# A layer kernel on one core: queries and keys stored split, and three output tiles moved beside the last attention head

## The chip, the cores and the metric

The kernel runs on one core of a Trainium2 chip. A core has five engines that work at the same time and each execute their own list of instructions strictly in order: TensorE (PE, matrix products), VectorE (DVE), ScalarE (ACT), GpSimd (POOL) and SyncE (SP, which here only issues transfers). They wait for each other through semaphores. The metric is the device time of one execution in microseconds, as the median of several.

## The reference, cut to what matters

One transformer-like layer over x (1024 tokens of 1024 numbers) and mem (256 tokens), all in float32:

```python
h = rms_norm(x, mix_pre_g)
u, q, k, v, f_logit = split(h @ w_in)            # 512 | 8 heads x 64, three times | 8
y_ssm = s5_mixer(u, ...)                         # state-space scan, gelu, gated linear unit
y_fox = forgetting_attention(q, k, v, f_logit)   # causal softmax attention with a decay bias
y_mix = concat([rms_norm(y_ssm, ssm_out_g), rms_norm(y_fox, fox_out_g)])
x = x + rms_norm(y_mix @ w_out, mix_post_g)
h = rms_norm(x, xa_pre_g)
x = x + rms_norm(memory_cross_attention(h, rms_norm(mem, mem_g), xa_wq, xa_wkv, xa_wo), xa_post_g)
h = rms_norm(x, ffn_pre_g)
x = x + rms_norm((silu(h @ w_gate) * (h @ w_up)) @ w_down, ffn_post_g)
```

## The kernel before, in words

**Precision.** Each factor of a product is split into a high part (a copy to the format fp32r, on ACT, L114) and the remainder (a subtraction on DVE, L116, or with a gain L118); `split` does this. `mm3` (L123 to L125) then makes one product out of three: high x high, high x low, low x high. So every operand costs ACT and DVE an instruction before PE may use it.

**Stages.** From 0 to about 185 us the input projection: u, then k, v, q in tiles of 128 columns by 1024 tokens (`qk_tile`, evacuated by L289), with the constants of the state-space branch (SSM) computed beside it on DVE (L505 to L621). To 222 the SSM's output (L638). From 222 to 500 the attention (`fox`). From 500 to 580 the output projection and the rest of the cross-attention's preparation, to 772 the cross-attention, to 1195 the first two products of the feed-forward part, and then the last.

**Attention.** `fox` goes through 64 units: 8 heads of 8 token tiles t, each of 128 rows against the 128(t+1) columns that causality leaves. A unit is: scores on PE (L734, L735), with a causal mask added (L737), into one of two two-bank PSUM buffers s; bias and minimum on DVE (L741); exponential on ACT (L743); reciprocal (L744) and normalisation, on DVE (L748) or, for t = 1, 3, 5 of heads 2 to 7, on POOL (L746); two units later transposes on PE (L765), evacuated by ACT or DVE (L770, L768); and after every pair of tiles of two heads the values' product (L779), whose squares are added up in `totals` (L789 to L793). `prepare(h)` loads one head's q and k from DRAM (qk_d, L714 and L715) in halves, and splits them: ACT L718 and L114, subtractions L719 and L116 on DVE for heads 0 and 1, on POOL for the others.

**Work beside it.** `fillers` is a second generator of PE work: the rest of v, the gated linear unit (`glu`), the SSM half of the output projection (`out_ssm`, L845, whose weights are in_w_out_s and whose result goes to DRAM as t1_d by L849), the memory tokens' normalisation (`mem_load`, L967), their 16 key and value tiles (`mem_tile`, evacuated by L979, stored as kv_d by L980), and `build_a(0)`, half of the product of the cross-attention's query weights with the keys. `paced` steps it at RATE steps per unit:

```python
    def paced(main, *side):
        for n, _ in enumerate(main):
            for gen, first, rate in side:
                if n >= first:
                    step(gen, int((n + 1 - first) * rate) - int((n - first) * rate))
```

Behind the attention come the attention half of the output projection (weights w_out_f[0] to [3], loaded by L1034 into the two buffers raw; eight token tiles; L1054 adds t1 back, L1062 adds the residual), and between its half tiles steps of `build_a(1)`.

**What sets the order.** The program is written as such generators, and a scheduler then fixes one order for each engine from the order of the code, priorities and the buffers that are free: raw has 2 buffers, whl (split weights) 3, slab 16, g in PSUM 4, s 2; t2 3, and a, b two each in the pool of temporaries, e and d one. `behind()` holds an instruction back until the last exponential that the code has issued. What the order doesn't move is waited for on the chip. Weights and reloaded intermediates are loaded through SP's queue, stores go through POOL's, except for t1_d and kv_d, which SP stores.

Of the kernel before, what the change touches and what calls it, by code (L numbers as in the profile page):

```python
# [17 lines left out]
P = 128  # L18
# [17 lines left out]
POOL_T = (1, 3, 5)  # L36
RATE = 1.02
# [4 lines left out]
OPB = 10  # L42
WARM = 11
# [10 lines left out]
def layer(ctx: ExitStack, tc: tile.TileContext, a, out):  # L54
# [95 lines left out]
    stA, stB, stC = pool, sp, pool  # L150
# [4 lines left out]
    def load_w(src, shape, first=0, stage=None):  # L155
        w = tt(stage, [P, D]) if stage else raw([P, D])
        hl = whl([P, 2, D])
        if not first:
            sp.dma_start(out=w, in_=src)
# [19 lines left out]
    qk_d = dram.tile([8, P, S], F32, name="qk_d")  # L179
# [105 lines left out]
    def qk_tile(i, xH, xL, rb, ahead=False):  # L285
        o = tt("a")
# [6 lines left out]
        stA.dma_start(out=qk_d[i], in_=o)  # L293
# [402 lines left out]

    def fox(yf):
        heads, units, pts = {}, {}, {}
        sv = const.tile([P, NT], F32, name="sv_f")

        def prepare(h):
            r0 = (h % 2) * 64
            qs = tt("a", [P, S], F32R)
            ka = slab([P, 2, S])
            ncb = tt("b")
            sp.dma_start(out=ncb, in_=nc_d[h:h + 1, :].broadcast_to([P, S]))
            heads[h] = (qs, ka, ncb)
            eng = dve if h < 2 else pool
            for hf in range(2):
                hs = slice(hf * 512, hf * 512 + 512)  # L710
                qk = tt("d" if h == 0 and hf else "e", [P, 2, 512])
                qd, kd = qk[:, 0], qk[:, 1]
                for rr in (0, 64):
                    sp.dma_start(out=qd[rr:rr + 64], in_=qk_d[h // 2, r0:r0 + 64, hs])  # L714
                    sp.dma_start(out=kd[rr:rr + 64], in_=qk_d[4 + h // 2, r0:r0 + 64, hs])  # L715
                yield
                with behind():
                    act.activation(out=qs[:, hs], in_=qd, func=AF.Copy)  # L718
                    eng.tensor_tensor(out=qs[64:128, hs], in0=qd[64:128], in1=qs[64:128, hs].bitcast(F32),  # L719
                                      op=ALU.subtract)  # L720
                    split(ka[:, 0, hs], ka[:, 1, hs], kd, lo_eng=eng)

        def behind():
            return tc.issue_after(last[-1].ins) if last else ExitStack()

        def scores(h, t):
# [18 lines left out]
            if t in POOL_T and h > 1:  # L745
                pool.tensor_tensor(out=sc[:, :ke], in0=sc[:, :ke], in1=rl.broadcast_to([P, ke]), op=ALU.mult)  # L746
            else:
                dve.tensor_scalar(out=sc[:, :ke], in0=sc[:, :ke], scalar1=rl, scalar2=None, op0=ALU.mult)  # L748
# [23 lines left out]
        def values(hp, qc):  # L772
# [28 lines left out]
        totals = []  # L801
# [22 lines left out]
        token_sums(sv, totals[0])  # L824
        rsqrt_mean(r_f, sv, 512)
# [133 lines left out]
    def mem_load(r, out):  # L959
# [23 lines left out]
    def fillers():  # L983
# [13 lines left out]
        yield from build_a(0)  # L997
# [3 lines left out]
    def build_a(c):  # L1001
        for t in range(2):
            Ah[c, t], Al[c, t] = slab([P, 4, 512]), slab([P, 4, 512])
        for h in range(2):
# [3 lines left out]
            kh = tt("ea"[h * (1 - c)], [P, 2, 2, 256], F32R)  # L1008
# [3 lines left out]
            for ft in range(0, KT, 2):  # L1012
# [611 lines left out]
```

## Time and profile before

| | |
|---|---|
| median of 3 runs | 1417.2 us (1416.4, 1417.2, 1421.53) |
| the profiled execution: its own time | 1418.95 us |
| its span, first to last instruction | 1417.2 us |
| mean granted clock of TensorE | 0.990 |

By stage, from windows of the trace (us of busy time; clock is the granted share of TensorE's full clock):

| stage | us | PE | DVE | ACT | POOL | clock |
|---|---|---|---|---|---|---|
| input projection, 0 to 185 | 185 | 182.2 | 151.8 | 89.0 | 11.4 | 1.00 |
| SSM output, to 222 | 37 | 35.9 | 8.3 | 16.5 | 3.4 | 1.00 |
| attention, to 500 | 278 | 259.9 | 185.8 | 182.3 | 65.2 | 0.96 |
| output projection, to 580 | 80 | 75.2 | 62.9 | 49.0 | 27.0 | 0.98 |
| cross-attention, to 772 | 192 | 191.5 | 101.6 | 72.7 | 23.3 | 1.00 |
| gate and up, to 1195 | 423 | 422.5 | 306.1 | 156.5 | 253.8 | 1.00 |
| down, to the end | 222 | 214.9 | 132.1 | 92.6 | 19.2 | 0.99 |

In the profile's rows an instruction is named by its engine, its line in the kernel and its operands as out<-in with the program's tile names; xN counts instructions. "idle before <-releaser" is the time in which the engine stood still ahead of it, and the instruction or transfer (DMA) that ended this.

### The profile page before, as it was taken

Reading aid. Unit: us, or ns where it says so; the run is one execution under the profiler, and the core shown is the slowest. Engines: PE = TensorE matmul, PEld = TensorE weight load, DVE = VectorE, ACT = ScalarE, POOL = GpSimd, SP = SyncE. Lnnn points to the kernel's source line nnn. Section 1 sums busy time; section 2 is a strip of 40 time slices with the busy share of each in tenths; the row PEclk is TensorE's granted clock in tenths of the full one; section 3 lists DMA queues with packets and bytes.
Section 4 is the critical chain, followed back from the end, with each engine's and each line's share of the span. In section 5 each row is a group of like instructions: output and inputs, shape, how many; then the busy total and the mean of one; then the engine's idle time right before and its main releaser. Section 6 shows DMA issues by size and latency. Waiting matters only on the chain.

```text
span 1417.2 us, 20364 instructions
## 1 busy us (share of the span) xinstructions
PE 1382.1 (98%) x7353; PEld 1162.5 (82%) x7353; DVE 948.5 (67%) x1693; ACT 658.7 (46%) x1305; POOL 403.2 (28%) x424
## 2 busy tenths in 40 slices
PE   9999999899899898999999999999999999999997
PEld 7889898689789686888888888888888888888886
DVE  8939937946566677636457677777776676555566
ACT  7372347866566555434334533333333334544441
POOL 0001000113243134002021467676666661000021
PEclk9999999899999999999999999999999999999999
DMA  6225554246543756024457255554444546955544
GB/s 216 91 90 136 156 179 130 75 148 188 182 129 103 198 178 220 15 75 148 164 179 266 98 186 186 185 186 149 149 156 156 171 149 234 346 207 191 180 163 164
DMA packets 109366, 231.07 MB, mean 163 GB/s; under 512 B 11720, under 2 KB 46536, under 8 KB 109136
## 3 DMA queue, kind: packets, MB, share of 16 engines
q1 hardware_dynamic: 94064, 178.34, 39.4%
q0 software_dynamic: 15200, 51.42, 10.2%
q8 instruction: 58, 0.95, 0.3%
q14 instruction: 44, 0.36, 0.1%
HBM read 165.23 MB, written 73.14 MB: 168 GB/s over the span
## 4 chain that ended last, share of the span: by engine, by line
PE 59%; DVE 1%; ACT 0%; issue 0%; DVEq 0%; ACTq 0%
PE x L1289 17%; PE g L1289 13%; PE x L1552 7%; PE g L1552 7%; PE x L125 2%; PE x L124 2%; PE x L123 2%; PE g L123 2%; PE g L125 2%; PE g L124 2%; PE g L1074 1%; PE g L1185 1%; DVE slab L116 0%; DVE whl L116 0%; DVE c L1062 0%
## 5 line engine op out<-in xcount | busy, mean ns | idle before, releaser
L1289 PE MATMUL x<-slab,op 128*128 128x512 f32 x984 | 233.2, 389 | 0.5 <-DVE op L116 0.5
L1289 PEld LDWEIGHTS x<-slab,op 128*128 128x128 f32 x984 | 184.6, 188 | 39.3 <-DVE op L116 1.0
L1289 PE MATMUL g<-slab,op 128*128 128x512 f32 x744 | 178.7, 389 | 0.0
L116 DVE TENSOR_TENSOR slab<-slab 128x1024 fp32r<-128x1024 f32 (+2 forms) x92 | 110.3, 1207 | 86.7 <-ACT slab L114 84.8
L1289 PEld LDWEIGHTS g<-slab,op 128*128 128x128 f32 x744 | 139.6, 188 | 29.0
L123 PE MATMUL g<-slab,whl 128*128 128x512 f32 (+1 forms) x416 | 151.7, 365 | 1.1 <-ACT t L979 0.7
L125 PE MATMUL g<-slab,whl 128*128 128x512 f32 (+1 forms) x416 | 148.7, 358 | 0.0
L124 PE MATMUL g<-slab,whl 128*128 128x512 f32 (+1 forms) x416 | 148.4, 357 | 0.0
L114 ACT ACTIVATE slab<-slab 128x1024 fp32r<-128x1024 f32 (+2 forms) x92 | 94.9, 1037 | 106.3 <-DMA slab<-hs_d 82.7
L1552 PE MATMUL g<-slab 128*128 128x512 f32 x462 | 126.6, 389 | 0.0
L1552 PE MATMUL x<-slab 128*128 128x512 f32 x462 | 126.6, 389 | 0.0
L1552 PEld LDWEIGHTS x<-slab 128*128 128x128 f32 x462 | 86.7, 188 | 18.0
L1552 PEld LDWEIGHTS g<-slab 128*128 128x128 f32 x462 | 86.7, 188 | 18.0
L116 DVE TENSOR_TENSOR whl<-raw,whl 128x1024 fp32r<-128x1024 f32 (+2 forms) x61 | 71.1, 1168 | 36.7 <-ACT whl L114 36.5
L116 DVE TENSOR_TENSOR op<-slab,op 128x512 fp32r<-128x512 f32 x80 | 86.4, 1091 | 11.6 <-ACT op L114 11.4
L123 PE MATMUL g<-whl,slab 128*128 128x256 f32 (+2 forms) x288 | 86.1, 307 | 5.0 <-ACT t L845 3.4
L123 PEld LDWEIGHTS g<-slab,whl 128*128 128x128 f32 x416 | 78.6, 189 | 12.2 <-ACT t L979 0.9
L125 PEld LDWEIGHTS g<-slab,whl 128*128 128x128 f32 x416 | 78.4, 189 | 11.8 <-DVE whl L116 0.2
L1365 POOL TENSOR_TENSOR wt<-wt 128x256 f32<-128x256 f32 x88 | 81.8, 930 | 19.6 <-DMA wt<-in_w_down 16.1
L124 PEld LDWEIGHTS g<-slab,whl 128*128 128x128 f32 x416 | 78.6, 189 | 10.6
L114 ACT ACTIVATE op<-slab 128x512 fp32r<-128x512 f32 x80 | 50.0, 627 | 78.5 <-PE x L1289 36.8
L124 PE MATMUL g<-whl,slab 128*128 128x256 f32 (+2 forms) x288 | 85.7, 298 | 0.0
(389 smaller groups left out, 2930.7 us busy)
## 6 DMA issues: line engine op xcount, KB each, us to landing
hs_d<-ev POOLq DMA_DIRECT2D x77, 256.0 KB, 2.6
slab<-hs_d SPq DMA_DIRECT2D x35, 512.0 KB
wt<-in_w_down SPq DMA_DIRECT2D x44, 256.0 KB
wt_d<-wt POOLq DMA_DIRECT2D x22, 512.0 KB, 4.7
slab<-in_w_gate SPq DMA_DIRECT2D x20, 512.0 KB
slab<-in_w_up SPq DMA_DIRECT2D x20, 512.0 KB
slab<-wt_d SPq DMA_DIRECT2D x20, 512.0 KB
wd_d<-in_w_down SPq DMA_DIRECT2D x33, 256.0 KB
```

The lines of the kernel that those rows point to most:

```text
L114: first = act.activation(out=hi, in_=src, func=AF.Copy, scale=1.0 if mul is None else mul)
L116: (lo_eng or dve).tensor_tensor(out=lo, in0=src, in1=hi.bitcast(F32), op=ALU.subtract)
L123: pe.matmul(ps, lh, rh, start=first, stop=False)
L124: pe.matmul(ps, lh, rl, start=False, stop=False)
L125: pe.matmul(ps, ll, rh, start=False, stop=last)
L1074: pe.transpose(tp[:, k], src[:, (k0 + k) * P:(k0 + k + 1) * P], ident)
L1185: turned = pe.transpose(tp[:, k], h3[:, (4 * n + k) * P:(4 * n + k + 1) * P], ident)
L1289: pe.matmul(ps, x[:, k], y[:, k], start=first and k + n == 0, stop=k == 3 and n == 2, skip_group_check=not first)
L1365: pool.tensor_tensor(out=o, in0=x, in1=y, op=ALU.subtract)
L1552: pe.matmul(banks[n][j], xo[:, u, js], wo[:, v], start=ends[0] and k == 0, stop=ends[1] and k == 2, skip_group_check=onto is not None)
```

## The change

1. `qk_d` holds q and k split, 2 x 128 x 1024 for each tile in place of 128 x 1024. `qk_tile` splits each half tile (high part into a t2 buffer, remainder in place) and stores three pieces, not one, through POOL's queue. `prepare` is left with loads alone: two for q, two for k per head.
2. `POOL_T` goes: DVE does all normalisations (now L743).
3. `stB` is POOL: the 32 stores of t1_d and kv_d leave SP's queue.
4. The weights w_out_f (`out_weights`) and the first three output tiles, 3, 4 and 5 (`out_tiles`), are now the last steps of `fillers`, each begun once the last head has given the token tiles that it needs (`ready`). The token sums are formed by parts (`out_scale`), and the end of a tile (`out_finish`) is written apart, for the first three behind the attention. `build_a(0)` is gone from the fillers; `both_a` runs both halves between the remaining five tiles.
5. `behind()` now also holds back the memory tokens' scaling and split (now L962), the splits of w_out_f and of build_a's products, and a few staged loads. The totals move to buffer e, as do all key splits of build_a; RATE is 0.98.

```diff
-POOL_T = (1, 3, 5)
-RATE = 1.02
+RATE = 0.98
...
+OUT_ORDER = (3, 4, 5, 6, 7, 0, 1, 2)
+EARLY = 3
...
-    stA, stB, stC = pool, sp, pool
+    stA, stB, stC = pool, pool, pool
...
-            sp.dma_start(out=w, in_=src)
+            with behind() if stage else ExitStack():
+                sp.dma_start(out=w, in_=src)
...
+    qk_d = dram.tile([8, 2, P, S], F32, name="qk_d")
...
     def qk_tile(i, xH, xL, rb, ahead=False):
-        o = tt("a")
+        hl = tt("a", [P, S], F32R)
+        o = hl.bitcast(F32)
...
         yield from proj_tile(load_w(a["w_f"][i], P), xH, xL, evac, ahead)
-        stA.dma_start(out=qk_d[i], in_=o)
+        for h in range(2):
+            hs = slice(h * 512, h * 512 + 512)
+            hi = t2t([P, 512], F32R)
+            split(hi, hl[:, hs], o[:, hs])
+            stA.dma_start(out=qk_d[i, 0, :, hs], in_=hi.bitcast(F32))
+        stA.dma_start(out=qk_d[i, 1], in_=o)
...
+    def behind():
+        return tc.issue_after(last[-1].ins)
...
-            eng = dve if h < 2 else pool
-            for hf in range(2):
...
-                    sp.dma_start(out=qd[rr:rr + 64], in_=qk_d[h // 2, r0:r0 + 64, hs])
-                    sp.dma_start(out=kd[rr:rr + 64], in_=qk_d[4 + h // 2, r0:r0 + 64, hs])
-                yield
-                with behind():
-                    act.activation(out=qs[:, hs], in_=qd, func=AF.Copy)
-                    eng.tensor_tensor(out=qs[64:128, hs], in0=qd[64:128], in1=qs[64:128, hs].bitcast(F32),
-                                      op=ALU.subtract)
-                    split(ka[:, 0, hs], ka[:, 1, hs], kd, lo_eng=eng)
-        def behind():
-            return tc.issue_after(last[-1].ins) if last else ExitStack()
+            q, k = qs.bitcast(F32), ka.bitcast(F32)
+            for t in range(2):
+                sp.dma_start(out=q[t * 64:t * 64 + 64], in_=qk_d[h // 2, t, r0:r0 + 64])
+            for rr in (0, 64):
+                sp.dma_start(out=k[rr:rr + 64], in_=qk_d[4 + h // 2, :, r0:r0 + 64].rearrange("t p s -> p t s"))
...
-            if t in POOL_T and h > 1:
-                pool.tensor_tensor(out=sc[:, :ke], in0=sc[:, :ke], in1=rl.broadcast_to([P, ke]), op=ALU.mult)
-            else:
-                dve.tensor_scalar(out=sc[:, :ke], in0=sc[:, :ke], scalar1=rl, scalar2=None, op0=ALU.mult)
+            dve.tensor_scalar(out=sc[:, :ke], in0=sc[:, :ke], scalar1=rl, scalar2=None, op0=ALU.mult)
...
-                    totals.append(tt("d"))
+                    totals.append(tt("e"))
...
-            split(yf[hp][:, 0, qs_], yf[hp][:, 1, qs_], yp, g_out[:, 4 + hp:5 + hp])
+            hi = split(yf[hp][:, 0, qs_], yf[hp][:, 1, qs_], yp, g_out[:, 4 + hp:5 + hp])
+            if (hp, qc) == (3, 3):
+                last.append(hi)
...
-        drain(prepare(0))
+        prepare(0)
...
-                    nxt = prepare(h + 1)
-                if t % 2 and h + 1 < NH:
-                    step(nxt)
+                    prepare(h + 1)
...
-        token_sums(sv, totals[0])
-        rsqrt_mean(r_f, sv, 512)
+                    if h == NH - 1:
+                        ready.append(t // 2)
...
             for kk in range(4):
-                dve.tensor_tensor(out=m[:, kk], in0=m[:, kk], in1=rb, op=ALU.mult)
-                split(mh[:, k + kk], ml[:, k + kk], m[:, kk], g_mem[:, k + kk:k + kk + 1])
+                with behind():
+                    dve.tensor_tensor(out=m[:, kk], in0=m[:, kk], in1=rb, op=ALU.mult)
+                    split(mh[:, k + kk], ml[:, k + kk], m[:, kk], g_mem[:, k + kk:k + kk + 1])
                 if kk % 2:
...
         yield from rows
-        yield from build_a(0)
+        yield from out_weights()
+        yield from out_tiles(OUT_ORDER[:EARLY], 0)
...
-            kh = tt("ea"[h * (1 - c)], [P, 2, 2, 256], F32R)
+            kh = tt("e", [P, 2, 2, 256], F32R)
             split(kh[:, 0], kh[:, 1], kr)
...
-                for f in range(2):
-                    split(Ah[c, ft // 4][:, ft % 4 + f, ms], Al[c, ft // 4][:, ft % 4 + f, ms], ps[:, f],
-                          g_xa[:, ft + f:ft + f + 1])
+                with behind():
+                    for f in range(2):
+                        done = split(Ah[c, ft // 4][:, ft % 4 + f, ms], Al[c, ft // 4][:, ft % 4 + f, ms], ps[:, f],
+                                     g_xa[:, ft + f:ft + f + 1])
                 yield
...
-    gp = fillers()
-    paced(fox(yf), (gp, 0, RATE))
-    drain(gp)
-    two.close()
-    psx = ctx.enter_context(tc.tile_pool(name="psx", bufs=4, space=PSUM))
+        last.append(done)
+    wo, kept, totals, ready, summed, unfinished = [], {}, [], [], [], []
+    sv_f = const.tile([P, NT], F32, name="sv_f")
...
-        return psx.tile(shape, F32, name="x", tag="x")
-    wo = []
-    for i in range(4):
-        w = raw([P, D])
-        sp.dma_start(out=w, in_=a["w_out_f"][i])
-        hl = slab([P, 2, D])
-        split(hl[:, 0], hl[:, 1], w)
-        wo.append(hl)
...
-    a1 = build_a(1)
-    kept = {}
-    for n, j in enumerate((3, 4, 5, 6, 7, 0, 1, 2)):
...
+    def out_weights():
+        g_mp.append(gain_row(0, "d"))
+        for i in range(4):
+            w = raw([P, D])
+            sp.dma_start(out=w, in_=a["w_out_f"][i])
+            hl = slab([P, 2, D])
+            with behind():
+                split(hl[:, 0], hl[:, 1], w)
+            wo.append(hl)
+        yield
+    def out_scale(j):
+        g = max(j // 2, 1)
+        if g not in summed:
+            summed.append(g)
+            js = slice(0 if g == 1 else 2 * g, 2 * g + 2)
+            token_sums(sv_f[:, js], totals[0][:, js.start * P:js.stop * P])
+            rsqrt_mean(r_f[:, js], sv_f[:, js], 512)
+    def out_tiles(order, n0):
+        for n, j in enumerate(order, n0):
+            while max(j // 2, 1) not in ready:
+                yield
+            ts = slice(j * P, (j + 1) * P)
+            t = tt("aba"[n % 3])
+            for i in range(2):
+                sp.dma_start(out=t[64 * i:64 * i + 64], in_=t1_d.rearrange("j (k s) d -> s k j d", s=16)[2 * j + i])
+            ss4 = sm(4, "ss4")
+            for h in range(2):
+                hs = slice(h * 512, h * 512 + 512)
+                ps = x_ps([P, 512])
+                for k in range(4):
+                    mm3(ps, yf[k][:, 0, ts], yf[k][:, 1, ts], wo[k][:, 0, hs], wo[k][:, 1, hs], k == 0, k == 3)
+                out_scale(j)
+                dve.scalar_tensor_tensor(out=t[:, hs], in0=ps, scalar=r_f[:, j:j + 1], in1=t[:, hs], op0=ALU.mult, op1=ALU.add)
+                for q in range(2 * h, 2 * h + 2):
+                    act.activation(out=tt("yt", [P, 256]), in_=t[:, q * 256:q * 256 + 256], func=AF.Square,
+                                   accum_out=ss4[:, q:q + 1])
+                pool.tensor_tensor(out=t[:, hs], in0=t[:, hs], in1=g_mp[0][:, hs], op=ALU.mult)
+                if h == 0:
+                    yield
+            unfinished.append((j, t, ss4))
+            if psx:
+                out_finish()
+            yield
+    def out_finish():
+        j, t, ss4 = unfinished.pop(0)
...
-        t = tt("aab"[n % 3])
...
-            step(a1)
+        sp.dma_start(out=xt, in_=a["x"][j * P:(j + 1) * P, :])
...
+    def both_a():
+        yield from build_a(0)
+        yield from build_a(1)
+    psx, g_mp = None, []
+    gp = fillers()
+    paced(fox(yf), (gp, 0, RATE))
+    two.close()
+    psx = ctx.enter_context(tc.tile_pool(name="psx", bufs=4, space=PSUM))
+    drain(gp)
+    for j in (4, 6):
+        out_scale(j)
+    while unfinished:
+        out_finish()
+    a1 = both_a()
+    for _ in out_tiles(OUT_ORDER[EARLY:], EARLY):
+        step(a1)
     drain(a1)
```

How this moves the instructions is seen in each engine's order; lines of the changed kernel have other numbers (its L1030 is L1034 of before, L1003 L1007, L1052 L1047, L1075 L1044, L161 L159; L117 is L116, L119 L118, L624 to L627 are L616 to L619, L292 is L289, L739 L741, L962 L967).

First, SP's queue near the end of the attention, before: raw is a load of weights, the names with t1 and kv_d are the intermediates read back, b, a, c and t2 their buffers.

```order
L849 DMA t1_d_112<-t2_4930 128x2x256
L1034 DMA raw_5371<-in_w_out_f 128x1024
L1047 DMA b_5596<-t1_d_112 64x1x1024 x2
L1007 DMA t2_5621<-kv_d_113 128x2x256
L1220 DMA t2_6027<-kv_d_113 128x2x256
L1047 DMA a_5395<-t1_d_112 64x1x1024 x2
L1047 DMA b_5850<-t1_d_112 64x1x1024 x2
L1034 DMA raw_5376<-in_w_out_f 128x1024
L1220 DMA t2_6078<-kv_d_113 128x2x256
L1044 DMA c_5393<-in_x 128x1024
L1044 DMA c_5503<-in_x 128x1024
```

And in the changed kernel, the same place:

```order
L1030 DMA raw_5011<-in_w_out_f 128x1024
L1030 DMA raw_5016<-in_w_out_f 128x1024
L720 DMA a_4244<-qk_d_107 64x1024 x2
L716 DMA b_4246<-nc_d_111 128x1024
L722 DMA slab_4245<-qk_d_107 64x2x1024 x2
L720 DMA a_4571<-qk_d_107 64x1024 x2
L716 DMA b_4573<-nc_d_111 128x1024
L722 DMA slab_4572<-qk_d_107 64x2x1024 x2
L1003 DMA t2_5395<-kv_d_113 128x2x256
L1003 DMA t2_5592<-kv_d_113 128x2x256
L1052 DMA a_5088<-t1_d_112 64x1x1024 x2
L1052 DMA b_5187<-t1_d_112 64x1x1024 x2
```

Two of the four loads of w_out_f (L1030) now stand ahead of the loads for heads 6 and 7 (a, b, slab from qk_d and nc_d); the other two stand farther down, behind loads of t1_d for the output tiles.

Second, DVE's queue at the second head, before; L967 scales the memory tokens (raw), L741 is the reduction of the scores s:

```order
L967 TENSOR_TENSOR raw_2774<-raw_2774,t2_2736 128x256 x3
L678 SCALAR_TENSOR_TENSOR t2_2672<-t2_2671,t2_2672 128x512
L967 TENSOR_TENSOR raw_2774<-raw_2774,t2_2736 128x256
L967 TENSOR_TENSOR raw_2879<-raw_2879,t2_2736 128x256 x4
L741 ISA c_2821,nlr_2822<-s_2815,b_2282 128x768
L741 ISA nlr_2822 128x1
L118 SCALAR_TENSOR_TENSOR slab_2773<-raw_2774,gains_98,slab_2772 128x256 x3
L118 SCALAR_TENSOR_TENSOR slab_2604<-t2_2672,gains_98,slab_2604 128x512
L684 TENSOR_TENSOR d_2342<-d_2342,t2_2671 128x512
```

And changed (L962 scales, L739 reduces):

```order
L739 ISA c_2814,nlr_2815<-s_2808,b_2304 128x768
L739 ISA nlr_2815 128x1
L742 RECIPROCAL nlr_2769<-nlr_2769 128x1
L686 SCALAR_TENSOR_TENSOR t2_2721<-t2_2720,t2_2721 128x512
L962 TENSOR_TENSOR raw_2828<-raw_2828,t2_2780 128x256 x4
L962 TENSOR_TENSOR raw_2935<-raw_2935,t2_2780 128x256
L743 TENSOR_SCALAR c_2768<-c_2768,nlr_2769 128x640
L962 TENSOR_TENSOR raw_2935<-raw_2935,t2_2780 128x256 x3
L742 RECIPROCAL nlr_2815<-nlr_2815 128x1
```

The reduction of the 768-wide tile stood behind all eight scalings, and now stands ahead of them.

Third, DVE's queue at the end of the input projection, before; L616 to L619 belong to the SSM, L289 evacuates q, L116 splits weights (whl):

```order
L616 TENSOR_TENSOR b_1668<-c_121,c_123 128x896
L116 TENSOR_TENSOR whl_1892<-raw_1891,whl_1892 128x1024
L617 TENSOR_TENSOR b_1669<-c_121,c_123 128x896
L618 TENSOR_TENSOR b_1668<-b_1668,b_1669 128x896
L289 SCALAR_TENSOR_TENSOR a_1821<-g_1827,d_690 128x4x128
L619 TENSOR_TENSOR b_1668<-b_1668,slab_938 128x896
L289 SCALAR_TENSOR_TENSOR a_1821<-g_1853,d_690 128x4x128
L116 TENSOR_TENSOR whl_2333<-raw_2331,whl_2333 128x1024
```

And changed; L117 with operands a and t2 is a split of q:

```order
L117 TENSOR_TENSOR whl_1956<-raw_1955,whl_1956 128x1024
L626 TENSOR_TENSOR b_1692<-b_1692,b_1693 128x896
L117 TENSOR_TENSOR a_1810<-a_1810,t2_1868 128x512
L117 TENSOR_TENSOR a_1810<-a_1810,t2_1872 128x512
L627 TENSOR_TENSOR b_1692<-b_1692,slab_953 128x896
L624 TENSOR_TENSOR b_1700<-c_121,c_123 128x896
L292 SCALAR_TENSOR_TENSOR a_1877<-g_1883,d_690 128x4x128
L625 TENSOR_TENSOR b_1701<-c_121,c_123 128x896
L626 TENSOR_TENSOR b_1700<-b_1700,b_1701 128x896
L292 SCALAR_TENSOR_TENSOR a_1877<-g_1909,d_690 128x4x128
L627 TENSOR_TENSOR b_1700<-b_1700,slab_954 128x896
L117 TENSOR_TENSOR whl_2396<-raw_2394,whl_2396 128x1024
```

The two splits of the last q tile but one (a_1810) now stand among the SSM's instructions, ahead of its last two L627.

More of the change, by code (lines that the diff above doesn't have):

```diff
@@ L177, in row_bcast @@
         return rb
-    qk_d = dram.tile([8, P, S], F32, name="qk_d")
+    qk_d = dram.tile([8, 2, P, S], F32, name="qk_d")
     v_d = dram.tile([NT, P, 512], F32, name="v_d")
@@ L800, in fox @@
         seq = [(h, t) for h in range(NH) for t in range(NT)]
-        totals = []
         lag = 2
         vs = {}
-        drain(prepare(0))
+        prepare(0)
         load_v(0)
@@ L1040, in layer @@
-    kept = {}
-    for n, j in enumerate((3, 4, 5, 6, 7, 0, 1, 2)):
-        ts = slice(j * P, (j + 1) * P)
-        xt = tt("c")
-        sp.dma_start(out=xt, in_=a["x"][ts, :])
-        t = tt("aab"[n % 3])
-        for i in range(2):
-            sp.dma_start(out=t[64 * i:64 * i + 64], in_=t1_d.rearrange("j (k s) d -> s k j d", s=16)[2 * j + i])
-        ss4, ss, r = sm(4, "ss4"), sm(1, "ss"), sm(1, "r")
-        for h in range(2):
-            hs = slice(h * 512, h * 512 + 512)
-            ps = x_ps([P, 512])
-            for k in range(4):
-                mm3(ps, yf[k][:, 0, ts], yf[k][:, 1, ts], wo[k][:, 0, hs], wo[k][:, 1, hs], k == 0, k == 3)
-            dve.scalar_tensor_tensor(out=t[:, hs], in0=ps, scalar=r_f[:, j:j + 1], in1=t[:, hs], op0=ALU.mult, op1=ALU.add)
-            for q in range(2 * h, 2 * h + 2):
-                act.activation(out=tt("yt", [P, 256]), in_=t[:, q * 256:q * 256 + 256], func=AF.Square,
-                               accum_out=ss4[:, q:q + 1])
-            pool.tensor_tensor(out=t[:, hs], in0=t[:, hs], in1=g_mp[:, hs], op=ALU.mult)
-            step(a1)
+        last.append(done)
```

8 lines of the change are left out of this document (2 added, 6 removed).

## The prediction

> **What bounds the kernel now.** First the page: span, and how busy each engine is.
>
> ```profile
> span 1417.2 us, 20364 instructions
> PE 1382.1 (98%) x7353; PEld 1162.5 (82%) x7353; DVE 948.5 (67%) x1693; ACT 658.7 (46%) x1305; POOL 403.2 (28%) x424
> ```
>
> PE (TensorE) is busy for 1382.1 of 1417.2 us, so at most 35.1 us can be won by closing its gaps, and a little more where its clock fell. The change leaves PE's work alone; all it can do is close gaps or open them. So the second view is what PE waited for, longest first (total, times, longest).
>
> ```profile
> PE g L779 <- ACT t L979: 4.0, 1, 4.0
> PE g L123 <- ACT t L845: 3.4, 2, 2.4
> PE x L123 <- ACT slab L114: 3.2, 1, 3.2
> PE s L734 <- DVE nlr L741: 3.0, 1, 3.0
> PE x L123 <- DVE a L1054: 1.9, 2, 1.1
> PE x L123 <- ACT whl L114: 1.7, 1, 1.7
> ```
>
> All six lie in the attention or the output projection behind it. The third view, windows around them, gives place, engine load and granted clock (window; length, then busy time of PE, PEld, DVE, ACT, POOL; PEclk).
>
> ```profile
> 140.00:183.00 43.00, 43.00 (x217) 35.50 (x209) 42.77 (x90) 14.87 (x21) 2.13 (x4) 1.00 0.62 180
> 260.00:270.00 10.00, 6.98 (x52) 5.60 (x50) 9.91 (x21) 8.18 (x18) 2.66 (x2) 1.00 0.19 52
> 270.00:280.00 10.00, 8.22 (x33) 7.24 (x34) 9.97 (x23) 7.96 (x18) 3.44 (x2) 0.53 0.39 114
> 370.00:380.00 10.00, 10.00 (x76) 7.41 (x74) 3.15 (x11) 5.75 (x14) 2.72 (x4) 0.85 0.36 93
> 410.00:420.00 10.00, 7.61 (x63) 6.33 (x63) 6.34 (x15) 5.84 (x14) 5.16 (x4) 1.00 0.44 124
> 470.00:480.00 10.00, 8.38 (x66) 6.43 (x64) 5.68 (x12) 4.20 (x10) 0.76 (x1) 1.00 1.05 192
> 480.00:490.00 10.00, 6.80 (x20) 5.30 (x20) 4.96 (x8) 5.36 (x9) 1.51 (x1) 0.66 0.66 230
> 550.00:560.00 10.00, 6.95 (x29) 4.78 (x27) 5.32 (x11) 4.11 (x17) 4.33 (x4) 1.00 0.30 107
> 560.00:570.00 10.00, 9.03 (x32) 6.87 (x33) 9.88 (x15) 9.97 (x19) 0.21 (x1) 0.83 0.50 157
> ```
>
> A long gap costs twice: PE stands still, and then works at a lower clock: 0.53 from 270 on, 0.85 from 370, 0.66 from 480. Behind the 2.4 us wait at 412 the clock stayed at 1.00. [...]
>
> The fourth view, the timeline, says why ACT and DVE were late (start, length, instruction, idle time ahead and its releaser).
>
> ```profile
> 367.79 1.06 ACT L114 ACTIVATE whl<-raw 128x1024 fp32r<-128x1024 f32 x1 [5.76 <-DMA raw<-in_w_out_s]
> 413.32 0.63 ACT L718 ACTIVATE a<-e 128x512 fp32r<-128x512 f32 x1 [3.14 <-DMA e<-qk_d]
> 482.30 1.06 ACT L114 ACTIVATE slab<-raw 128x1024 fp32r<-128x1024 f32 x1 [6.70 <-DMA raw<-in_w_out_f]
> 555.01 0.75 DVE L1054 SCALAR_TENSOR_TENSOR a<-x,r_f,a 128x512 f32<-128x512 f32 x1 [2.64 <-DMA a<-t_d]
> ```
>
> Each is an engine that executes in order and stands at an instruction whose data is still being loaded, while PE's evacuations queue behind it. Only the gap at 267 (L734) has another cause: DVE is full (9.91 and 9.97 of 10 us).
>
> **The change part by part.** 1. *q and k are stored split.* The prices:
>
> ```profile
> e<-qk_d SPq DMA_DIRECT2D x60, 128.0 KB
> L289 DVE SCALAR_TENSOR_TENSOR a<-g,d 128x512 f32<-128x512 f32 x16 | 17.6, 1130 | 14.1 <-PE g L125 14.1
> L116 DVE TENSOR_TENSOR slab<-g,slab 128x512 fp32r<-128x512 f32 x1 | 0.7, 683 | 0.0
> L719 POOL TENSOR_TENSOR a<-e,a 64x512 fp32r<-64x512 f32 x12 | 16.1, 1341 | 51.3 <-ACT a L718 50.7
> L116 POOL TENSOR_TENSOR slab<-e,slab 128x512 fp32r<-128x512 f32 x12 | 19.3, 1612 | 3.3 <-ACT slab L114 2.6
> ```
>
> Removed in the attention: 32 ACT copies, 24 POOL subtractions (35.4 us), 8 on DVE, and 64 small loads on SP's queue for 32 larger ones. Added in the input projection: 16 copies on ACT, which is at 14.87 of 43 us, so nothing; 16 subtractions on DVE, 16 x 0.683 = 10.9 us. Half (q, done last) falls between 140 and 183, where DVE is full (42.77 of 43): 5.5 us that push the SSM's chain and the weight splits back.
>
> ```profile
> 182.15 1.11 DVE L619 TENSOR_TENSOR b<-b,slab 128x896 f32<-128x896 f32 x1
> 183.16 1.14 DVE L289 SCALAR_TENSOR_TENSOR a<-g,d 128x512 f32<-128x512 f32 x1
> 186.32 1.23 DVE L116 TENSOR_TENSOR whl<-raw,whl 128x1024 fp32r<-128x1024 f32 x1 [2.02 <-ACT whl L114]
> 199.05 0.69 DVE L719 TENSOR_TENSOR a<-e,a 64x512 fp32r<-64x512 f32 x1 [11.51 <-ACT a L718]
> ```
>
> Behind 184.3 DVE idles 2.0 and then 11.5 us, which takes up 5.5 us of delay. What the last L619 makes belongs to the SSM's second half, used after the first; the v weights' split is nearer to its use. I take **+1 us**, bounds 0 (all in the slack) and +10.9 (none). What this wins: the wait at 413.32 was for a load of qk_d that is now no longer converted, so ACT does not stop there: **-2.4**. If another load takes its place on ACT, 0.
>
> 2. *Normalisations on DVE alone, no longer on POOL for three of eight tiles.*
>
> ```profile
> L746 POOL TENSOR_TENSOR c<-c,nlr 128x768 f32<-128x768 f32 x6 | 8.8, 1467 | 18.2 <-DVE nlr L744 15.3 <-PE g L779 2.8
> L748 DVE TENSOR_SCALAR c<-c,nlr 128x640 f32<-128x640 f32 x8 | 6.7, 841 | 0.2
> L748 DVE TENSOR_SCALAR c<-c,nlr 128x1024 f32<-128x1024 f32 x8 | 6.0, 751 | 0.2
> L748 DVE TENSOR_SCALAR c<-c,nlr 128x512 f32<-128x512 f32 x2 | 1.0, 478 | 0.0
> L748 DVE TENSOR_SCALAR c<-c,nlr 128x256 f32<-128x256 f32 x2 | 0.7, 352 | 0.0
> ```
>
> DVE takes 18 more: 6 x (0.352 + 0.478 + at most 0.751) = 9.5 us at most. But the 640-wide one (841 ns) takes longer than the 1024-wide (751 ns), so something beside it slows it, and POOL's work stands next to it; with POOL idle, 640 wide should lie between 478 and 751, which gives back 8 x about 0.2 us, and the other DVE operations gain too. DVE is 67% busy over the span, and where it is full (part 4) the moved ones only begin later, with head 2, so: 0. [...]
>
> 3. *SP's queue loses 32 stores to POOL's, and the loads move.*
>
> ```profile
> 356.49 0.38 SPq L797 DMA_DIRECT2D slab<-v_d  x1
> 356.97 0.52 SPq L980 DMA_DIRECT2D kv_d<-t  x1
> 358.26 1.70 SPq L159 DMA_DIRECT2D raw<-in_w_out_s  x1
> ```
>
> The load that ACT awaited at 367.79 was issued at 358.26, behind a 1 MB load of v and a store that itself waits for ACT's evacuation (L979); 9.5 us passed from issue to use. Without stores on SP, and with this weight load ahead of v's, it should come some us earlier; ACT then waits little. At stake are 4.0 us, and 10 x 0.15 = 1.5 at the lower clock; I take three quarters of 5.5, **-4.1** (bounds 0 and -5.5). POOL's queue now holds these stores behind its additions of squares (L790), and they free the three t2 tiles that ACT evacuates into; the 35.4 us taken off POOL in part 1 leave room for them.
>
> 4. *Memory tokens' scaling held back.* In DVE's order the reduction for which PE waited 3.0 us now stands ahead of the eight scalings that preceded it: **-3.0**. At 0.53, 10 us of work lost 4.7; smaller gaps remain there, so I take a third, **-1.5**. Bounds: -9.5 (all 4.8 us idle between 260 and 280, and the 4.7) and +3 (an equal wait on another reduction). At the start of attention, however, five score tiles, 128 to 640 wide, now stand in PE's order without v's matmuls between them, and two buffers hold them, so each waits for a reduction on DVE.
>
> ```profile
> L741 DVE CUSTOM_DVE_ANT_0 c<-s,b 128x640 f32<-128x640 f32 x8 | 6.6, 823 | 5.7 <-PE s L737 4.2 <-POOL d L793 1.4
> ```
>
> Three such waits of at most 0.8 us: **+1.5** (0 to +2.5).
>
> 5. *Three output tiles beside the last head, key product behind.* Idle from 470 to 490 and 550 to 570: 1.62 + 3.20 + 3.05 + 0.97 = 8.8 us, and 3.4 + 1.7 at the lower clock (10 us each at 0.66 and 0.83): 13.9. The weights w_out_f[0] and [1] are now loaded before head 6, so the first of them cannot make PE wait; [2] and [3] stand behind a load that waits for the last scores, and ACT's splits of them stand ahead of evacuations. PE has whole tiles of work before it needs them. Eight long tiles mixed with the products should also cover the t1 loads of 555. I take three quarters, **-10.5** (0 to -13.9), and for the new waits, namely ACT at weights [2] or [3], and the key split in buffer e, which now waits for the last token sums, **+3** (0 to +6.7, ACT's longest wait of that kind above).
>
> Sum: 1 - 2.4 - 4.1 - 4.5 + 1.5 - 10.5 + 3 = **-16.0 us**. The profiled execution took 1418.95 us (span 1417.2 and 1.75 around it); its time lies 1.75 above the median of the runs shown, within their 1416.4 to 1421.5. So 1418.95 - 16.0 = 1403, or 1401 from the median; I say **1402**.
>
> **The rivals.**
> *A, gains handed on (no change that can be measured).* Around 464-580 DVE works
>
> ```profile
> 464.00:580.00 116.00, 106.41 (x581) 87.06 (x580) 83.58 (x152) 67.30 (x174) 30.99 (x26) 0.96 0.61 182
> ```
>
> 83.6 of 116 us, and already 9.88 of 10 at 560. With both key products gathered at its end and not spread over the attention, DVE can become the bound there, as can ACT standing at w_out_f[2] or [3] for its 6.7 us, with a lower clock after it (3.4). Then part 5 gives -10.5 + 6.7 + 3.4 = -0.4, the other parts as above -8.5, and a new wait on DVE like that of 267 +3.0: -5.9, that is **1413**. For it: four ACT or DVE waits on loads now, of which the change removes two only by earlier issue. Against: 8 long tiles are easier to interleave than short ones.
> *B, slower.* The input projection: DVE is full there and PE is not idle at all (43.00 of 43), so a delay that outruns the buffers shows whole: +10.9 us in place of +1, and a stretch at half clock as at 270 (+4.7). With A's -5.9 that is +8.7, **1428**. It decides once DVE's delay at the v weights' split exceeds what lies between split and use; the 13.5 us of idle DVE behind 184.3 speak against it.
> *C, more.* All identified gaps and clock stretches go: 9.5 + 5.5 + 2.4 + 13.9 less 2.5 of costs (the +1 and +1.5), -28.8: **1390**.
>
> **How the numbers follow.** 0.5% is 7.1 us, about what a measurement of this kernel can tell from no change: faster is below 1410, slower above 1424 (from the median). Forecast 0.60, C 0.11, A 0.18, B 0.11. So faster 0.71, same 0.18, slower 0.11. The range takes in forecast, A, and most of C, and leaves out B and the end of C: 1387 to 1417.
>
> **What would show it.** Right: PE's list of waits without L779's 4.0, with no ACT wait on qk_d, and none over 2 us on reductions at 267; windows 260-290, 370-380 (shifted) and 470-490 at clock 1.00; DVE idle still present between the q tiles and the attention. Wrong: a PE wait on DVE's split or on ACT before 220 (B); an ACT idle of over 5 us ended by raw<-in_w_out_f, or DVE above 9.5 of 10 through the products (A).

## The result: slower by 0.8%

The changed kernel takes 1430.5 us (median of four runs, 1427.4 to 1432.8), the kernel before 1416.8 beside it. The ratio is 1.0081, with a 95% interval of 1.0062 to 1.0100: 9 to 14 us slower, where 16 faster were forecast. The profiled execution is the fastest of the four, 1427.4 us; the traces below therefore show 8.5 us of the loss.

Page of the changed kernel, the rows that were read first of before:

```profile
span 1425.6 us, 20283 instructions
PE 1381.9 (97%) x7353; PEld 1163.6 (82%) x7353; DVE 949.1 (67%) x1729; ACT 652.1 (46%) x1293; POOL 380.3 (27%) x430
```

PE's own work is the same to 0.2 us; what changed is what it waits for. Its waits, changed kernel (total, times, longest):

```profile
PE g L124 <- ACT e L115: 10.0, 3, 6.7
PE g L124 <- ACT slab L115: 7.8, 1, 7.8
PE g L124 <- ACT t L974: 3.5, 2, 2.4
PE g L125 <- DVE e L117: 3.0, 2, 2.0
PE g L240 <- ACT slab L765: 1.9, 1, 1.9
PE g L646 <- DMA slab<-T_d: 1.6, 1, 1.6
```

Of the six waits listed of before, the one of 4.0 us on L979 (now L974) has shrunk to 2.4, and those on a reduction (3.0) and on the converted q and k have gone. But three rows are new, and their 20.8 us are more than the 17.2 of all six of before: a weight split (slab L115, 7.8) and the key split (e, 10.0 on ACT and 3.0 on DVE). First the two windows at 270 and 370 that had been slow before, in the changed kernel (columns as in the prediction; behind PEclk stand the busy share of the 16 DMA engines and the GB/s that they moved):

```profile
270.00:280.00 10.00, 7.68 (x47) 6.33 (x47) 9.83 (x25) 7.86 (x18) 0.00 (x0) 0.79 0.35 88
370.00:380.00 10.00, 10.00 (x84) 8.07 (x83) 5.65 (x18) 5.97 (x16) 2.14 (x3) 1.00 0.44 145
```

And the windows around the new waits:

```profile
460.00:465.00 5.00, 5.00 (x31) 4.30 (x30) 1.97 (x4) 0.77 (x2) 1.29 (x1) 1.00 0.94 206
465.00:470.00 5.00, 0.66 (x6) 0.41 (x5) 0.00 (x0) 0.00 (x0) 0.00 (x0) 0.69 0.97 206
470.00:475.00 5.00, 1.55 (x5) 1.37 (x6) 1.47 (x3) 1.06 (x1) 0.00 (x0) 0.50 0.50 164
535.00:540.00 5.00, 0.00 (x0) 0.00 (x0) 4.17 (x7) 3.47 (x10) 1.26 (x1) 0.86 0.78 276
540.00:545.00 5.00, 2.35 (x9) 2.06 (x10) 4.96 (x9) 3.58 (x15) 3.43 (x2) 0.50 0.63 188
```

From 465.7 to 472.3 every engine stands still and only the transfers go on, with a DMA share of 0.97 in the row of 465 to 470: the kernel waits for a load and for nothing else. What arrived then, from the timelines of ACT and DVE:

```profile
472.34 1.06 ACT L115 ACTIVATE slab<-raw 128x1024 fp32r<-128x1024 f32 x1 [10.75 <-DMA raw<-in_w_out_f]
535.75 1.41 DVE L1060 SCALAR_TENSOR_TENSOR a<-x,r_f,a 128x512 f32<-128x512 f32 x2 [4.30 <-DMA a<-t_d]
536.53 0.42 ACT L1062 ACTIVATE yt<-a 128x256 f32<-128x256 f32 x1 [4.22 <-DVE a L1060]
```

And when it had been asked for, from SP's queue:

```profile
454.96 1.30 SPq L1052 DMA_DIRECT2D a<-t_d  x2
456.36 1.20 SPq L1052 DMA_DIRECT2D b<-t_d  x2
457.67 1.19 SPq L1052 DMA_DIRECT2D a<-t_d  x2
458.96 0.39 SPq L1030 DMA_DIRECT2D raw<-in_w_out_f  x1
459.39 1.21 SPq L1052 DMA_DIRECT2D b<-t_d  x2
```

The load of w_out_f[2] was issued at 458.96 and used at 472.34: 13.4 us for 512 KB, amid four token tiles of t1 (2 MB, t_d in these rows), which could only start when the last t1 store, issued at 451.5, had landed (SP waits 4.9 us for it). At 535 the same shows in small: DVE stands at a t1 load (issued at 526.99), ACT behind DVE, and the key split, on which PE waits 6.7 us, behind both in ACT's order.

Where the time came and went, by the start of the same instruction in both traces:

| | before | changed | difference |
|---|---|---|---|
| SSM output's first product | 185.7 | 189.4 | +3.7 |
| last score tile of head 5 | 411.9 | 407.4 | -4.5 |
| first transposes of the cross-attention | 574.7 | 583.5 | +8.8 |
| end of PE's work | 1409.9 | 1418.3 | +8.4 |

So the input projection lost 3.7, the attention up to there won 8.2, and from there to the cross-attention 13.3 us were lost. Some 2 us of the last two are work put off, not won and lost: with RATE at 0.98 the changed kernel has 13 matrix products fewer behind it at head 5's last score tile than the kernel before (1595 against 1608 since the SSM output's first).

### The profile page after: what moved, and what is told of

Its sections match the earlier page's. It is cut to its first block, busy times and chain, and to the rows that moved or that the text cites. A ratio compares the mean times of both kernels' runs of the same rounds, so it can differ in the third digit from the quotient of the medians.

```text
span 1425.6 us, 20283 instructions
## 1 busy us (share of the span) xinstructions
PE 1381.9 (97%) x7353; PEld 1163.6 (82%) x7353; DVE 949.1 (67%) x1729; ACT 652.1 (46%) x1293; POOL 380.3 (27%) x430
## 4 chain that ended last, share of the span: by engine, by line
PE 81%; DVE 8%; DMA 6%; ACT 3%; issue 2%; SPq 0%; DVEq 0%; POOL 0%; ACTq 0%; POOLq 0%
PE x L1322 17%; PE g L1322 13%; PE x L1585 7%; PE g L1585 7%; PE g L124 6%; PE g L125 6%; PE g L126 6%; PE x L125 2%; PE x L126 2%; PE x L124 2%; PE g L774 2%; PE g L760 2%; DVE whl L117 1%; PE s L732 1%; PE s L733 1%
## 5 line engine op out<-in xcount | busy, mean ns | idle before, releaser
L117 DVE TENSOR_TENSOR slab<-slab 128x1024 fp32r<-128x1024 f32 (+2 forms) x92 | 110.3, 1207 | 85.4 <-ACT slab L115 83.6
L115 ACT ACTIVATE slab<-slab 128x1024 fp32r<-128x1024 f32 (+2 forms) x92 | 95.0, 1037 | 104.2 <-DMA slab<-hs_d 75.1
L117 DVE TENSOR_TENSOR op<-slab,op 128x512 fp32r<-128x512 f32 x80 | 86.6, 1093 | 10.4 <-ACT op L115 10.2
L1398 POOL TENSOR_TENSOR wt<-wt 128x256 f32<-128x256 f32 x88 | 84.2, 957 | 25.2 <-DMA wt<-in_w_down 15.1
L117 DVE TENSOR_TENSOR whl<-raw,whl 128x1024 fp32r<-128x1024 f32 (+2 forms) x61 | 68.5, 1129 | 33.3 <-ACT whl L115 32.8
L115 ACT ACTIVATE op<-slab 128x512 fp32r<-128x512 f32 x80 | 49.9, 628 | 78.6 <-PE g L1322 37.9
```

What stands on the lines that cost most here:

```text
L115: first = act.activation(out=hi, in_=src, func=AF.Copy, scale=1.0 if mul is None else mul)
L117: (lo_eng or dve).tensor_tensor(out=lo, in0=src, in1=hi.bitcast(F32), op=ALU.subtract)
L1398: pool.tensor_tensor(out=o, in0=x, in1=y, op=ALU.subtract)
```

## The experiments

The parts are numbered as in the prediction. Theory **T**: part 5 (early output tiles, key product behind, and with them RATE) carries the loss. Rival **B**: the input projection and the stores carry it. Each ratio is to the kernel before on the same chip.

**Part 5 undone, and part 5 alone.** The first restores the old order in the changed kernel:

```diff
-        yield from out_weights()
-        yield from out_tiles(OUT_ORDER[:EARLY], 0)
+        yield from build_a(0)
...
-RATE = 0.98
+RATE = 1.02
```

> Part 5 undone alone: build_a(0) back among the fillers, all eight output tiles behind the attention, RATE 1.02; q and k stay stored split, POOL_T stays gone, stores stay on POOL, the memory tokens' scaling stays held back. Theory T (part 5 carries the loss: up to the score tiles of head 5 the changed kernel is 4.5 us ahead of before, and 8.8 us behind where the cross-attention starts, so part 5 costs 13): about 1412 us, 4 to 5 faster than before. Rival B (the input projection and the stores carry it): still slower than before, 1420 to 1430.

Measured: 1417.0 us, ratio 0.9983 (0.9969 to 0.9998): faster than before, as T has it, but by 2.4 us and not by 4 to 5. The second puts the new order alone on the kernel before (the inverse of this diff, with the new functions):

> Part 5 alone on the kernel before (early output tiles, weights w_out_f beside the last head, both key products behind, RATE 0.98; q and k converted in the attention as before, so that the totals sit in buffer d, and the post gain in e). Theory T: 1417 + 13 = 1430 us, with a wait of PE on w_out_f[2] of 5 us or more and one on the key split. Rival B: 1417 or less.

Measured: 1432.7 us, ratio 1.0090 (1.0063 to 1.0116). T holds on both sides: part 5 costs 0.98% (1.0081 less 0.9983), about 14 us, on the other parts, and 0.9% or 13 us without them. In the waits of part 5 alone the same two stand out, the first of them larger (10.4 in place of 7.8):

```profile
PE g L125 <- ACT slab L116: 11.1, 2, 10.4
PE g L125 <- ACT d L116: 9.7, 3, 6.3
```

The next runs ask why part 5 costs so much.

**Weight splits not held back.**

```diff
-            with behind():
-                split(hl[:, 0], hl[:, 1], w)
+            split(hl[:, 0], hl[:, 1], w)
```

> The changed kernel, but the splits of w_out_f are not held behind the last exponential, so the load of w_out_f[2] stands one load of t1 ahead of its old place, and [3] one or two. Theory T: the wait of 7.8 us at 465 shrinks to under 3 and the low clock behind it (about 5 us) goes: 1418 to 1423 us. If the transfers are only limited by their sum (DMA share 0.94 to 0.97 there), the wait moves to the t1 loads and the time stays at 1428 to 1431. Rival B: 1430.

Measured: 1434.5 us (1430.5 to 1440.2), ratio 1.0099 (1.0066 to 1.0132). A miss for the order of loads: in the trace, which is of the slowest of its four executions (1440.2), the wait shrank to 5.4, and others of 2.7 and 2.2 took its place.

**Two buffers for the key split.**

```diff
-            kh = tt("e", [P, 2, 2, 256], F32R)
+            kh = tt("eb"[h], [P, 2, 2, 256], F32R)
```

> The changed kernel, but the key split alternates between buffer e and buffer b. Theory T: the waits of PE on the key split (6.7 + 2.0 at 534, 2.6 + 1.1 at 551) lose at least the second pair: 1424 to 1427 us; if the single buffer made both and the half clock behind them, 1415 to 1419. Rival B: 1430.

Measured: 1425.3 us, ratio 1.0033 (1.0016 to 1.0051), so about 7 us less than the changed kernel's 1.0081. The waits on the key split fell from 13.0 to 0.7; what remains behind the attention is

```profile
PE g L124 <- ACT slab L115: 8.9, 2, 8.5
PE g L124 <- DVE slab L119: 4.2, 3, 2.1
```

The single buffer was worth half of part 5's price: with one, a head's keys can only be split when the last product of the head before is through (528.5 in the changed kernel), and the split came at 539.99, behind the output tile's squares (L1062) in ACT's order.

**Weights [2] and [3] loaded ahead of t1.** Two theories of the 7.8 us wait: T1, the order of the loads; T2, their volume.

```diff
+        two_w = slab([P, 2, D], F32)
         for i in range(4):
-            w = raw([P, D])
+            w = raw([P, D]) if i < 2 else two_w[:, i - 2]
```

> The changed kernel, but w_out_f[2] and [3] are loaded into one free slab, not into the two raw buffers once these are split, and so ahead of the loads of t1. Theory T1 (the 7.8 us wait at 465 and the half clock behind it come from the order of these loads): that wait falls under 2 us, no low clock there: 1430 - 12 = 1417 to 1420 us. Theory T2 (the transfers as a whole are too much for that stretch, DMA share 0.97): PE waits as long for the t1 loads instead, 1428 to 1431.

Measured: 1431.9 us, ratio 1.0092 (1.0072 to 1.0112). T1 falls. All four weights were split by 467.5, and yet PE waits as long:

```profile
PE g L124 <- DVE sv_f L241: 9.1, 1, 9.1
```

The releaser is a copy of token sums that costs 0.15 us; its own reason is in ACT's timeline of the same run:

```profile
480.05 1.06 ACT L115 ACTIVATE whl<-raw 128x1024 fp32r<-128x1024 f32 x1 [14.48 <-DMA raw<-in_wqT]
```

Now it is the next weights, of the key product, that ACT and DVE stand at, while the evacuations that PE needs queue behind them. Two of their loads, issued at 465.61 and 468.43, stand among the t1 loads where those of w_out_f had been, so the stretch has as much to move as before. What is loaded last there is what is waited for: w_out_f[2] in the changed kernel (7.8 us), the key product's weights here (9.1).

**Both mends.**

> The changed kernel with both: w_out_f[2] and [3] staged in a slab, and the key split alternating between buffers e and b. If part 5 lost its time by just these two waits: 1430 - 12 - 5 = 1411 to 1414 us, faster than before. If the rest of part 5 (loads of t1 on which DVE stands, products without output tiles between them) costs too: 1416 to 1420.

Measured: 1426.3 us, ratio 1.0045 (1.0029 to 1.0061), above both ranges: the second key buffer's gain, and nothing from the staging.

**SSM rows ahead of the memory tiles.** This takes volume out of the stretch: t1 is complete some 40 us sooner, and the first two output tiles' parts of it are read while heads 6 and 7 still run.

```diff
+        yield from rows
         for i in range(16):
             mem_tile(i, *mem)
             yield
-        yield from rows
```

> The changed kernel, but the SSM half of the output projection (out_ssm) stands ahead of the 16 memory tiles in the fillers, so that the last store of t1_d comes some 40 us earlier and the first two output tiles' t1 can be loaded while head 7 runs. Theory T2 (2 MB of t1 and 1 MB of weights asked for at once at 455, when the last t1 store is done, are too much for that stretch): 1 MB leaves it, the wait of 8 us at 465 falls to 0 to 4 and the half clock behind it goes: 1418 to 1424 us. If the order of loads alone decides: 1430.

Measured: 1421.9 us, ratio 1.0026 (1.0012 to 1.0041), 8 us better than the changed kernel; the wait for the weight split is 4.3 in place of 7.8. The low clock behind it has not gone (0.60 from 465 to 470).

**Half of t1.**

```diff
-                sp.dma_start(out=t[64 * i:64 * i + 64], ...
+                sp.dma_start(out=t[64 * i:64 * i + 64, 0:512], ...
```

> The changed kernel, loading only the first 512 of 1024 columns of t1 for each output tile; it leaves out the SSM half's addend in the other columns (a scaling on DVE in place of the addition). Theory T2: 1 MB less between 455 and 475, and shorter loads for the tiles behind on which DVE and ACT stood at 521 and 535: 1415 to 1422 us. If not the volume but the order of waits decides: 1428 to 1431.

Measured: 1417.8 us, ratio 0.9996 (0.9980 to 1.0012). The window from 455 to 480, PE's busy time in the changed kernel, and in this one:

```profile
455.00:480.00 25.00, 17.20 (x87) 13.71 (x84) 10.52 (x21) 7.95 (x16) 3.05 (x2) 0.80 0.71 197
```

```profile
455.00:480.00 25.00, 24.52 (x147) 18.85 (x147) 18.06 (x32) 14.00 (x27) 3.40 (x3) 1.00 0.63 206
```

PE is busy 24.5 of 25 us at full clock, in place of 17.2 at 0.80. The stretch lost more than the 1 MB that isn't loaded: the first halves of t1 were stored earlier, so two of the four half tiles were loaded at 437.77 and 439.15, and after 455 only two stood in the queue, 0.5 MB in place of 2 MB. T2 holds on both of its tests, read as what is asked for in that stretch; neither separates the bytes from the late start of their loads, behind the last t1 store.

**All mends.** The rows first, the staged weights and the second key buffer:

> The same with w_out_f[2] and [3] staged in a slab and the key split in two buffers. Theory T2: 1426 (both mends without it) less 8 to 12: 1414 to 1418 us. If what was left of part 5's loss is elsewhere: 1422 to 1426.

Measured: 1414.6 us, ratio 0.9968 (0.9952 to 0.9983). It is about 16 us better than the change as it was made (1.0081 less 0.9968), and 0.3% better than before; only part 1 alone, below, comes as low. Its largest waits:

```profile
PE g L124 <- DVE slab L119: 5.5, 3, 2.3
PE g L124 <- DVE sv_f L241: 3.3, 1, 3.3
```

**Part 1 alone**, on the kernel before (the diff's `qk_tile` and `prepare`, nothing else):

> Part 1 alone on the kernel before: q and k stored split in the input projection, and loaded by the attention without conversion. The changed kernel's SSM output began 3.7 us later than before; if that is this part's price and the attention gives back only the wait at 412 (2.4): 1417 to 1420 us. If the 35 us taken off POOL and the ACT copies free more (the reductions at 267 too): 1411 to 1414.

Measured: 1414.8 us, ratio 0.9976 (0.9963 to 0.9990). It holds as much of the gain as parts 1 to 4 together (0.9983); the intervals overlap. The SSM output begins at 188.2 (+2.5), the last score tile of head 5 at 408.7.

**Part 3 undone** too, in the kernel without part 5 (`stA, stB, stC = pool, sp, pool`):

> The kernel with part 5 undone, with t1_d and kv_d stored through SP's queue again (part 3 undone too). If part 3 won what was forecast, the wait for w_out_s at 365 returns (4.0 us and 1.5 at the lower clock): 1421 to 1423 us against the 1417 with part 3. [...]

Measured: 1418.1 us, ratio 0.9992 (0.9980 to 1.0004), against 0.9983 with part 3: the intervals overlap, so it can't be told whether the stores' queue is worth anything, and the 4.0 us wait did not come back. The expectation was not met. Nor do parts 2 and 4 show a gain: this kernel holds them beside part 1, which alone is at 0.9976.

**The splits of part 1 on POOL.**

```diff
-            split(hi, hl[:, hs], o[:, hs])
+            split(hi, hl[:, hs], o[:, hs], lo_eng=pool)
```

> Part 1 alone (1414.8 us), with the 16 subtractions in the input projection done by POOL, not DVE. If DVE's 10.9 us are what delays the SSM output by 2.5 us there: 1412 to 1413 us. If POOL's work slows DVE's beside it by as much as it takes off it (640 wide: 841 against 634 ns): 1414 to 1416; worse than that, 1417 or more.

Measured: 1433.1 us, ratio 1.0111 (1.0088 to 1.0134), far beyond the first two ranges: the third case, worse than that. DVE does such a subtraction in 686 ns (first row, part 1 alone). POOL's mean in this kernel is 2355 ns (second row), but that is the mean of eleven that took 1.3 to 1.6 us, and of one that took 13.08:

```profile
L116 DVE TENSOR_TENSOR a<-a,t 128x512 fp32r<-128x512 f32 x15 | 9.9, 686 | 3.2 <-ACT t L114 3.2
```

```profile
L116 POOL TENSOR_TENSOR a<-a,t 128x512 fp32r<-128x512 f32 x12 | 28.3, 2355 | 62.8 <-ACT t L114 62.7
```

```profile
117.41 13.08 POOL L116 TENSOR_TENSOR a<-a,t 128x512 fp32r<-128x512 f32 x1 [12.51 <-ACT t L114]
128.96 0.41 DVE L561 TENSOR_TENSOR slab<-slab,b 128x256 f32<-128x256 f32 x1
```

DVE works without a pause from 106.5 to the end of the last row, 129.4; POOL's subtraction ends 1.1 us after that. The t2 buffers, freed by stores in POOL's own queue behind it, hold up ACT, and ACT holds up PE by 9.0 us:

```profile
132.92 0.47 ACT L317 ACTIVATE t<-g,r_x 128x256 f32<-128x256 f32 x1 [14.57 <-DMA qk_d<-t]
```

## Why the prediction was wrong, point by point

**Part 5 is the step that failed**: forecast at -10.5 and +3 for its new waits, -7.5 in all, it cost 13 to 14 us. Two sentences were wrong. "PE has whole tiles of work before it needs them", said of w_out_f[2] and [3]: these loads were indeed what ACT waited for, as named, but their price was bounded by ACT's longest wait of before (6.7 us), although such a load stood in a full stretch even then. The row of 470 to 480 of before, quoted in the prediction, shows a DMA share of 1.05, which the prediction does not use. That wait of 6.7 us, at 482.30, was for this load of w_out_f[1], behind three token tiles of t1:

```profile
467.86 1.19 SPq L1047 DMA_DIRECT2D b<-t_d  x2
469.15 0.39 SPq L1034 DMA_DIRECT2D raw<-in_w_out_f  x1
```

So 13.2 us passed from issue to use before the change, and 13.4 after it. The new order asks there for four tiles of t1 and two weights, 3 MB; at the 206 GB/s of that stretch this gives an estimate of 15 us. In the kernel before, build_a(0) gave PE work at that place (PE is busy for the whole of 475 to 480), and PE waited 3.2 us; the change took this work away, and PE waited 7.8. And the key split "in buffer e, which now waits for the last token sums" was priced with the rest in the +3: its single buffer cost about 7 us by itself, since every head's split also waits for the products of the head before.

**Rival A** had the place and both mechanisms (ACT at the weights, low clock after), and was too cheap: it had part 5 at -0.4. **Rival B** had the sign and, by luck, nearly the time (1428), for its cause was another: the input projection cost 3.7 us, not 10.9 and a half-clock stretch. Its mechanism was there, at a third of its price, and did not decide.

**The input projection, +1**: measured +3.7 in the changed kernel and +2.5 with part 1 alone. PE did not wait for the v weights, as I had supposed, but for the load of the SSM's matrix T, which comes from DVE's chain (SP issues it at 183.18, when DVE's L627 ends; before, at 177.05):

```profile
189.44 0.46 PE L646 MATMUL g<-slab 128*128 128x128 f32 x2 [1.65 <-DMA slab<-T_d]
```

So DVE's delay is 6.1 us, where 5.5 were forecast. The idle time behind 184.3 that was counted as slack lies for the most part after the use of T, at 185.7 in the kernel before. This wait is 1.65 of the 3.7; PE also stands still 1.6 us more between 60 and 140 (busy 77.1 of 80 in place of 78.7), and why stays open. The mechanism was named, the size was three times too small, within its bounds.

**The attention, -9.5 for parts 1, 3 and 4 with the start's +1.5**: -8.2 by the table, but part 5's RATE is in that: part 5 alone reaches head 5's last score tile at 409.8, 2.1 sooner than before, though its SSM output begins at the same time (185.6). In the kernel without part 5 this stretch takes 219.6 us against 226.2, so parts 1 to 4 won 6.6, two thirds of the forecast; and part 1 alone, of which -2.4 was expected here, won 5.7 of them (220.5). The conversions' wait (-2.4) went. The wait at 365 (-4.1) shrank by 1.6 in the changed kernel and its low clock went, but part 3 had little to do with it: with part 1 alone, and the stores on SP, PE is busy at full clock from 360 to 380, with half as many loads of q and k in SP's queue. At 267 the wait of 3.0 became the same 2.0 with part 1 alone and with parts 1 to 4 (first and second row: part 1 alone, without part 5), and the clock behind it is 0.50 from 275 to 280 in both, so holding back the scaling (part 4) shows no gain of its own:

```profile
PE s L728 <- DVE nlr L735: 3.5, 3, 2.0
PE s L732 <- DVE nlr L739: 3.5, 3, 2.0
```

Only in the changed kernel, with all five parts, does this wait go; 1.9 on another came (L240), and the clock from 270 to 280 is 0.79 against 0.53. The start's +1.5 did not show; head 0's score tiles take 15.1 us against 16.1.

**The normalisations, 0**: right as far as it can be told. The row by which I suspected POOL's work beside it is borne out: with the subtractions gone from POOL, but POOL_T kept, DVE's 640-wide normalisation falls from 841 to 634 ns.

```profile
L742 DVE TENSOR_SCALAR c<-c,nlr 128x896 f32<-128x896 f32 x8 | 5.5, 684 | 0.2
L742 DVE TENSOR_SCALAR c<-c,nlr 128x640 f32<-128x640 f32 x8 | 5.1, 634 | 0.2
```

Single executions in the kernel before show how: the five of eight beside which POOL did nothing took 0.55 to 0.56 us, the three that met an operation of POOL 1.18 to 1.39, as at 343:

```profile
342.21 2.16 POOL L116 TENSOR_TENSOR slab<-e,slab 128x512 fp32r<-128x512 f32 x1
343.32 1.39 DVE L748 TENSOR_SCALAR c<-c,nlr 128x640 f32<-128x640 f32 x1
```

**The clock**: what the prediction read from its windows, that a long gap is followed by a lower clock, shows again: behind the new waits of 7.8 and 6.7 us the clock is 0.50 from 470 to 475 and from 540 to 545. The prediction used it for the gains and left it out of the new waits' price. But the length of the gap alone does not decide. Before, the clock stayed at 1.00 from 410 to 420, around the wait of 2.4 us at 412; in the changed kernel one of 1.85 us was followed by 0.50:

```profile
274.58 1.05 PE L240 MATMUL g<-ones,d 128*128 128x1 f32 x8 [1.85 <-ACT slab L765]
276.00:282.00 6.00, 5.53 (x26) 5.09 (x25) 4.90 (x16) 4.04 (x11) 0.00 (x0) 0.50 0.59 180
```

What decides beside the length, no run here shows.

What stays open: why the loads of t1 move only 206 GB/s at a DMA share of 0.97, when 309 GB/s passed at 0.80 from 475 to 480. That their rows are taken from two token groups is not needed for it: the loads of one head's keys, which like those of t1 go into 64 partitions each but take their rows in order, move no more when they are alone (first row). The other row is of loads into 128 partitions, of x and of weights:

```profile
251.00:254.00 3.00, 3.00 (x21) 2.50 (x20) 1.81 (x7) 2.09 (x4) 0.00 (x0) 1.00 1.04 216
476.00:478.00 2.00, 2.00 (x8) 1.65 (x7) 0.24 (x1) 1.33 (x3) 0.00 (x0) 0.72 1.02 386
```

So the 64 partitions are the likely cause; no run loads t1 into 128 at once.

## What to carry to other kernels

When a step is moved, add up the bytes that its loads bring to the new place and divide by the rate that the trace shows for loads of that shape. Here 3 MB at 206 GB/s came to an estimate of 15 us, in a stretch whose DMA share was 0.94 to 0.97, and two other orders of its loads left waits of 5.4 and 9.1 us where there had been 7.8. In such a stretch an engine that executes in order passes the wait on to what stands behind it (ACT's 14.48 us at a load of weights became PE's 9.1 on a copy of 0.15), so look for the load behind the releaser, not at the releaser. And each buffer that a moved step shares with its own next round can be a wait per round: with one key buffer PE waited 13.0 us for the key split, with two 0.7.

## What the hardware showed that was not expected

A subtraction of 128 x 512 took 686 ns on DVE and mostly 1.3 to 1.6 us on POOL, but once 13.08 us, where DVE worked beside it without a pause; it ended 1.1 us after that stretch of DVE's. Moving 16 such subtractions from DVE (11 us) to POOL made the kernel 19 us slower (1.0111 less 0.9976). At the same share of busy time, 1.02 to 1.04, the transfers moved 216 GB/s into 64 partitions at a time and 386 into 128. And the clock fell to one half behind a gap of 1.85 us, and not behind one of 2.4.
